# A fused transformer block on one Trainium2 core: when the row-finishing work of the second feed-forward product is issued, and the order of two products in the last up column tile

## The chip, the cores and the metric

The kernel runs on one core of one Trainium2 chip. The metric is the device time of one execution in microseconds. The kernel before took 1763.22 us in the median of three runs (1759.53 to 1764.78).

## The reference, cut to what matters

One hybrid block: a modulated norm, attention and a recurrent mixer, a merge through `w_o`, and then a feed-forward part with a convolution along the rows, all in float32 on 1024 rows by 1024 columns. The change lies in the feed-forward part and the final norm:

```python
def conv_ffn(u, w_up, conv_w, conv_b, w_down):       # u [1024,1024], w_up [1024, 2*2816], w_down [2816,1024]
    a, b = jnp.split(u @ w_up, 2, axis=-1)
    a = lax.conv_general_dilated(a, ...) + conv_b    # width 3, causal, per column
    return (jax.nn.silu(a) * b) @ w_down
...
    h = h + gate2[:, None, :] * conv_ffn(u2, w_up[l], conv_w[l], conv_b[l], w_down[l])
    return rms_norm(h, final_g)                      # per row: y * rsqrt(mean(y*y) + eps) * final_g
```

## The kernel before, in words

**Products.** Every matrix product is done with seven half-size block products (Strassen's scheme in Winograd's form) instead of eight, called P1 to P7 in this document and `k` in the code. Each float32 operand is split into a rounded high part and a rest (`split`: ScalarE casts the high part, line 1298; VectorE subtracts for the rest, line 1301), and one product of operands takes three matmuls (`PARTS`: high by high, low by high, high by low, in this order).

**Up product.** It runs over 22 column tiles (`NFF`), i = 0 to 21. `plan` (lines 1556 to 1560) writes out the order of (tile, product) by hand. For tiles from 3 on this is P1, P7, then P3 of the tile before, then P6, P2, P4, P5. P1, P6, P5 and P3 of a tile add up in one PSUM bank, called X; P7 and P4 in the bank Y; P2 in W. `up_evac` reads a bank after a product: after P6 a copy U of X is taken (line 1510), after P4 `U = Y + U` (line 1515), after P5 `Z = X + Z` (line 1517, reading X), after P3 X is copied (line 1519) and fed to the convolution (lines 1478, 1475, 1482). P3 writes X again, so it must come after line 1517 has read it. In tiles up to 20, P1 and P7 of the next tile lie between P5 and P3; in tile 21 nothing does.

**Second product.** `ORDER = (1, 7, 6, 4, 5, 2, 3)` is the order of its seven block products, called stages s = 0 to 6. Each stage has 11 units (`NP`), so there are 77 units, u = 0 to 76. A unit is 12 matmuls: for each of four row blocks `tp`, three matmuls into that row block's bank. `dn_load` issues a unit's loads on the DMA queue of SyncE, `dn_make` its casts and subtractions; `dn_ahead(u + 8, u + 5)` keeps loads up to eight units and operands up to four units ahead of the unit that is multiplied. Operands lie in a ring of ten buffers (`RING`), two per unit, so the casts of unit u + 4 wait until TensorE has finished unit u - 1. The first units' loads and operands are made during tile 21 of the up product, by a table of `dn_ahead` arguments that is indexed by the product just finished.

**Order on the engines.** From line 1666 on the instructions of all engines stand in the order in which the program issues them. Each engine takes its own in that order.

**Finishing the rows.** The right half rows 512 to 1023 (`R`) are complete after stage 4. `row_sum` (VectorE lines 1758 and 1759, then ScalarE's squares with row sums, line 1760, and `rms_rstd`, lines 280 and 281) and `row_out` (VectorE line 1765, then the store, line 1766) finish one of four row blocks each. In stage 5 they are issued alternately, after units j = 1 to 8. Rows 0 to 511 have their left columns complete after stage 5 (`dn_evac`, line 1746); `first_left` (VectorE lines 1772 and 1773, ScalarE line 1774, VectorE lines 1775 and 1776) does one row block of these after each of the units j = 1 to 4 of stage 6.

**The last stage.** In stage 6 only the first `own = NP - 5`, that is six, units run unit by unit. The other five (u = 72 to 76) run row block by row block: 15 matmuls of row block 0, then `last_right(0)`, then 15 of row block 1, and so on. `last_right` is a chain through VectorE and ScalarE (lines 1782 to 1788) and ends with two stores.

Of the kernel before, what the change touches and what calls it, by code (L numbers as in the profile page):

```python
# [11 lines left out]
AF = mybir.ActivationFunctionType  # L12
ALU = mybir.AluOpType
# [5 lines left out]
NH = 512  # L19
FF = 2816  # L20
NFF = FF // 128
NP = NFF // 2
# [109 lines left out]
def hybrid_block(ctx: ExitStack, tc: tile.TileContext, a, out):  # L132
    nc = tc.nc
# [15 lines left out]
    tt, stt, ts = nc.vector.tensor_tensor, nc.vector.scalar_tensor_tensor, nc.vector.tensor_scalar  # L149
# [128 lines left out]
    def rms_rstd(dst, ssq):  # L278

        nc.scalar.activation(dst, ssq, AF.Ln, scale=1.0 / D, bias=epsr[:, 0:1])  # L280
        nc.scalar.activation(dst, dst, AF.Exp, scale=-0.5)
# [46 lines left out]
    with ExitStack() as es:  # L328
# [67 lines left out]
        with tc.tile_pool(name="st", bufs=1) as st, tc.tile_pool(name="stp", bufs=2, space=PS) as stp, \  # L396
                tc.manual_schedule(engines={mybir.EngineType.SP, mybir.EngineType.DVE, mybir.EngineType.Activation}):
            ssq = st.tile([128, 8], F32, name="ssq")
# [589 lines left out]
    with tc.manual_schedule(engines={mybir.EngineType.DVE, mybir.EngineType.Activation}):  # L988
# [6 lines left out]
        def slot(free):  # L995
            while not free:
                yield 100
            yield free.popleft() - weave.now
# [156 lines left out]
    def bank(k, name):  # L1155
        return pb.tile([128, NH], F32, tag="big", name=name) if k > 5 else pz.tile([128, NH], F32, tag=f"p{k}", name=name)
# [58 lines left out]
    with ExitStack() as es:  # L1215
# [24 lines left out]
        for n in range(8):  # L1240
            if n > 1:
                br_open(n)
            if n:
                for kt in ((n - 1,), (6, 7))[n == 7]:
                    i = nc.sync.dma_start(wo[kt], a["w_o"][kt * 128 : kt * 128 + 128, :])
# [17 lines left out]
    ssq = hp.tile([128, 32], F32, name="ssq2")  # L1263
# [241 lines left out]
    def up_evac(i, k):  # L1505
        o = ups[i]
        if k in (1, 7, 6):
            key = {1: "x1", 7: "Z", 6: "U"}[k]
            o[key] = hp.tile([128, NH], F32, tag="xq", name=f"{key}_{i}", bufs=5)
            nc.scalar.copy(o[key], o["Y" if k == 7 else "X"])  # L1510
        elif k == 2:
            if i > 1:
                up_first(i)
        elif k == 4:
            o["C21"] = tt(o["U"], o["Y"], o["U"], op=ALU.add)
        elif k == 5:
            o["C22"] = tt(o["Z"], o["X"], o["Z"], op=ALU.add)  # L1517
        else:
            nc.scalar.copy(o["ab"][:, 2 + NH :], o["X"])
            conv_last(i, 1, o["X"])  # L1520
            later(0, conv_taps, i, 1)
            later(1, silu, i, 1)
            later(2, gated, i, 1)
# [32 lines left out]
    plan = [(i, k) for ks in ((1, 2), (7,), (6,)) for i in range(2) for k in ks]  # L1556
    plan += [(0, 4), (0, 5), (1, 4), (1, 5), (0, 3), (1, 3)] + [(2, k) for k in (1, 7, 6, 2, 4, 5)]
    for i in range(3, NFF):
        plan += [(i, 1), (i, 7), (i - 1, 3)] + [(i, k) for k in (6, 2, 4, 5)]
    plan.append((NFF - 1, 3))  # L1560
    done = {"made": 0, "run": 0}

# [70 lines left out]
    for n in range(4):  # L1633
        i, k = next(steps)
# [49 lines left out]
    def dn_load(u):  # L1684
        k, j = units[u]
        if j % 2 == 0:
            n, w, r = AS.index(OPS[k][0]), min(2, NP - j), GR[dn["g"] % len(GR)]
            dn["g"] += 1
            graw[k, j] = rp.tile([128, 1024], F32, tag="raw", name=f"g{k}_{j}") if r[0] == "r" else slot(r, f"g{k}_{j}")
            nc.sync.dma_start(graw[k, j][:, 0 : w * NH].rearrange("p (j n) -> p j n", n=NH), d_g[n, :, j : j + w, :])  # L1690
        if k in (1, 7, 4):
            x, cs = {1: (0, slice(0, D)), 7: (1, slice(NH, D)), 4: (1, slice(0, NH))}[k]
            if (j, x) not in wd:
                wd[j, x] = slot(WR[x][j], f"wd{2 * j + x}")
            i = 2 * j + x
            nc.sync.dma_start(wd[j, x][:, cs], a["w_down"][i * 128 : i * 128 + 128, cs])
# [6 lines left out]
    def dn_ahead(loads, makes):  # L1703
        while dn["loaded"] < min(len(units), loads):
            dn_load(dn["loaded"])
            dn["loaded"] += 1
        while dn["made"] < min(len(units), makes):
            dn_make(dn["made"])
            dn["made"] += 1

    def dn_make(u):

        k, j = units[u]
        first, other = W_(j, "B11"), W_(j, "B12")
        if k in (7, 6, 4):
            x, y = {7: (W_(j, "B22"), other), 6: (W_(j, "B22"), first), 4: (W_(j, "B21"), other)}[k]
            tt(other, x, y, op=ALU.subtract)
            w = other
        else:
            w = first if k in (1, 5) else W_(j, OPS[k][1])  # L1720
        for x, src in enumerate((G_(k, j), w)):
            op = slot(RING[(2 * u + x) % 10], f"op{u}{x}", F32R)
            split(op[:, 0:NH], op[:, NH:], src, nc.vector)
            dn_ops[u, x] = op[:, 0:NH], op[:, NH:]
        if k == 1:
            tt(first, other, first, op=ALU.subtract)

    def dn_mm(u, tp, ps):
        k, j = units[u]
        (gs, ws) = (dn_ops[u, x] for x in range(2))  # L1730
        for n, (xi, wi) in enumerate(PARTS):
            mm(ps, gs[xi][:, tp * 128 : tp * 128 + 128], ws[wi], start=k in FRESH and j == 0 and n == 0,
               stop=j == NP - 1 and n == 2, more=k not in FRESH)

    def dn_evac(k, tp, ps):
        if k == 1:
            nc.scalar.copy(XT[tp], ps)
        elif k == 7:
            nc.scalar.copy(R[tp][:, NH:], ps)
        elif k == 6:  # L1740
            nc.scalar.copy(R[tp][:, 0:NH], ps)
        elif k in (4, 5):
            c = R[tp][:, 0:NH] if k == 4 else R[tp][:, NH:]
            tt(c, ps, c, op=ALU.add)
        elif k == 2:
            tt(XT[tp], ps, XT[tp], op=ALU.add)
        else:
            last_right(tp, ps)

    def h_back(t, tag):  # L1750
        H[t] = slot(tag, f"h{t}_")
        nc.sync.dma_start(H[t], d_h[t])
# [1 line left out]


    def row_sum(tp):
        t, x = 4 + tp, R[tp]
        tt(x, x, g2b, op=ALU.mult)
        tt(x, x, H[t], op=ALU.add)
        nc.scalar.activation(H[t], x, AF.Square, accum_out=ssq[:, t : t + 1])  # L1760
        rms_rstd(ssq[:, 16 + t : 17 + t], ssq[:, t : t + 1])

    def row_out(tp):
# [6 lines left out]
    def first_left(t):  # L1770
        x, h = XT[t], H[t][:, 0:NH]
        tt(x, x, g2b[:, 0:NH], op=ALU.mult)
        tt(h, h, x, op=ALU.add)
        nc.scalar.activation(x, h, AF.Square, accum_out=ssq[:, t : t + 1])
        ts(ssq[:, t : t + 1], ssq[:, t : t + 1], 1.0 / D, RMS_EPS, op0=ALU.mult, op1=ALU.add)
        tt(x, h, fgb[:, 0:NH], op=ALU.mult)

# [15 lines left out]
    for i, k in steps:  # L1793
        up_evac(i, k)
        if i == NFF - 1:
            dn_ahead(*{1: (0, 0), 7: (4, 0), 6: (4, 0), 2: (5, 1), 4: (6, 2), 5: (7, 3), 3: (8, 4)}[k])
    while due:
        done["run"] += 1
        run_due()
# [6 lines left out]
    XT = [slot(k, f"xt{k}") for k in ("b7", "e5")]  # L1806
    XT = [XT[tp // 2][:, tp % 2 * NH : tp % 2 * NH + NH] for tp in range(4)]
    R = [slot(f"h{4 + tp}", f"r{tp}") for tp in range(4)]
    H = {}
    banks = [bank(k, f"D{k}") for k in (2, 3, 4, 6, 0, 7, 5, 1)]  # L1810
    for s, k in enumerate(ORDER):
        ps = banks[4:] if k in (7, 4, 2) else banks[0:4]
        own = NP - 5 if s == 6 else NP
        for j in range(own):
            u = s * NP + j
            dn_ahead(u + 8, u + 5)
            for tp in range(4):
                dn_mm(u, tp, ps[tp])
            if s == 4 and j in (5, 6, 7, 8):
                h_back(j - 1, f"h{j - 5}")  # L1820
            if s == 5 and j < 4:
                h_back(j, f"m{12 + j}")
            if s == 5 and 1 <= j <= 8:
                (row_sum if j % 2 else row_out)((j - 1) // 2)
            if s == 6 and 1 <= j <= 4:
                first_left(j - 1)
        if s == 3:
            fgb = slot("e1", "fgb")
            nc.sync.dma_start(fgb, a["final_g"].to_broadcast([128, D]))
        if s == 6:  # L1830
            dn_ahead(len(units), len(units))
        for tp in range(4):
            for j in range(own, NP):
                dn_mm(s * NP + j, tp, ps[tp])
            dn_evac(k, tp, ps[tp])
# [78 lines left out]
```

## Time and profile before

| | us |
|---|---|
| median of three runs (lowest to highest) | 1763.22 (1759.53 to 1764.78) |
| the profiled execution's own time | 1764.5 |
| span of the profiled execution | 1762.4 |
| TensorE busy | 1660.7 (94% of the span) |
| VectorE busy | 1264.8 (72%) |
| ScalarE busy | 818.0 (46%) |
| GpSimd busy | 352.7 (20%), none of it in the stretch of this change |
| first matmul of the second product | 1531.14 after the start of the span |
| end of its last matmul | 1754.90 |

PE is TensorE's matmul, PEld its weight load, DVE is VectorE, ACT is ScalarE, SPq the DMA queue of SyncE. A row of a timeline gives the start and the duration in us, the engine, the line of the source, the operation, the tile written and the tiles read, the shape, the count of instructions merged into the row, and in brackets how long the engine was idle ahead of it and which instruction ended that. `[2.45 <-DVE Z L1517]` is an idle time of 2.45 us that ended when VectorE's line 1517 had written Z. A row of a table by windows gives the stretch, its length, the busy time and count for PE, PEld, DVE, ACT and POOL, then the clock granted to TensorE as a fraction, the busy share of the DMA engines and GB/s.

### The profile page before, as it was taken

To read this page: it belongs to the slowest core of one execution; us is meant where nothing else is said; L and a number is where in the kernel's file an instruction comes from. 1 tells how busy PE (TensorE), PEld (TensorE's weight loads), DVE (VectorE), ACT (ScalarE), POOL (GpSimd) and SP (SyncE) were. 2 spreads that over 40 slices of the span, in tenths; PEclk is the share of its full clock that TensorE was granted. 3 is DMA by queue.
4 is the path that set the end of the run, shared out by engine and by line. 5 is a ranking of instruction groups with operands and counts; after the bars stand their busy time and mean duration, and the time that the engine had idled before them with its cause. 6 is when DMAs were issued, how large, how long until landed. Compare 5 with 4: busy or idle time off the path is not lost.

```text
span 1762.4 us, 26237 instructions
## 1 busy us (share of the span) xinstructions
PE 1660.7 (94%) x9838; PEld 1353.2 (77%) x9838; DVE 1264.8 (72%) x2342; ACT 818.0 (46%) x1502; POOL 352.7 (20%) x249
## 2 busy tenths in 40 slices
PE   7999989999899997999899898999999999999997
PEld 7767767778687776888788777788888888788875
DVE  5765777777867424888649898877777777786576
ACT  5453234434334444767630335744444444445444
POOL 0233222332322222322138473000000000000000
PEclk9999989999999998999999899999999999999998
DMA  8487633442323229444168502122332322574442
GB/s 317 145 294 227 168 100 103 114 114 88 101 93 95 74 78 175 124 112 127 43 233 312 209 22 96 60 90 90 121 113 90 114 92 100 208 241 160 160 151 90
DMA packets 120846, 239.85 MB, mean 136 GB/s; under 512 B 39760, under 2 KB 48208, under 8 KB 120720
## 3 DMA queue, kind: packets, MB, share of 16 engines
q1 hardware_dynamic: 105600, 220.94, 38.4%
q0 software_dynamic: 15120, 17.25, 4.5%
q8 instruction: 77, 1.26, 0.3%
q14 instruction: 49, 0.40, 0.1%
HBM read 172.59 MB, written 65.54 MB: 135 GB/s over the span
## 4 chain that ended last, share of the span: by engine, by line
PE 60%; DVE 22%; DMA 8%; issue 5%; ACT 2%; POOL 1%; SPq 1%; DVEq 0%; ACTq 0%; POOLq 0%
PE X L140 13%; PE D L140 9%; PE Y L140 6%; PE rk_ps L140 4%; PE ps_rkv L140 4%; PE gt L140 3%; PE W L140 3%; DVE E L764 3%; DVE t L762 3%; PE qk L140 2%; PE lg L140 2%; DMA wm<-in_w_mod 2%; PE ov L140 2%; PE tp L144 2%; PE sp L140 1%
## 5 line engine op out<-in xcount | busy, mean ns | idle before, releaser
L140 PE MATMUL D<-op,op 128*128 128x512 f32 x924 | 216.0, 396 | 7.8 <-ACT op L1298 7.5
L140 PEld LDWEIGHTS D<-op,op 128*128 128x128 f32 x924 | 175.7, 191 | 47.9 <-ACT op L1298 8.8
L256 POOL TENSOR_TENSOR lo_in<-raw_in,hi_in 128x1024 fp32r<-128x1024 f32 x48 | 119.8, 2497 | 244.7 <-ACT hi_in L255 70.8
L140 PE MATMUL X<-T,S 128*128 128x512 f32 x528 | 127.1, 390 | 0.8 <-DVE T L1301 0.8
L140 PEld LDWEIGHTS X<-T,S 128*128 128x128 f32 x528 | 99.0, 188 | 21.9 <-DVE T L1301 1.4
L762 DVE TENSOR_TENSOR t<-E,M 128x60 f32<-128x60 f32 (+24 forms) x248 | 79.3, 320 | 29.6 <-DMA M<-sm 23.9
L1301 DVE TENSOR_TENSOR op<-g,op 128x512 fp32r<-128x512 f32 x77 | 53.0, 688 | 53.8 <-ACT op L1298 53.8
L1475 DVE SCALAR_TENSOR_TENSOR c<-ab,vec,c 128x512 f32<-128x512 f32 x88 | 65.9, 749 | 22.5 <-ACT c L1478 21.1
L1298 ACT CAST op<-g 128x512 fp32r<-128x512 f32 x77 | 47.6, 619 | 65.2 <-PE D L140 40.1
L1439 DVE TENSOR_TENSOR S<-ur,S 128x512 fp32r<-128x512 f32 x66 | 45.6, 691 | 39.0 <-ACT S L1435 39.0
L764 DVE TENSOR_TENSOR E<-E,t 128x60 f32<-128x60 f32 (+24 forms) x248 | 67.7, 273 | 5.9
L255 ACT CAST hi_in<-raw_in 128x1024 fp32r<-128x1024 f32 x40 | 41.8, 1046 | 62.3 <-PE ps_rkv L140 25.2
L1439 DVE TENSOR_TENSOR A<-ur,A 128x512 fp32r<-128x512 f32 x66 | 46.4, 704 | 32.2 <-ACT A L1435 32.2
L140 PE MATMUL X<-B,S 128*128 128x512 f32 x264 | 65.0, 397 | 2.5 <-DVE Z L1517 2.5
L140 PE MATMUL Y<-T,S 128*128 128x512 f32 x264 | 64.5, 391 | 2.6 <-ACT T L1298 1.3
L1435 ACT CAST S<-ur 128x512 fp32r<-128x512 f32 x66 | 41.0, 622 | 49.5 <-DVE ur L1426 31.0
L140 PE MATMUL X<-B,A 128*128 128x512 f32 x264 | 63.5, 390 | 0.0
L140 PE MATMUL W<-B,A 128*128 128x512 f32 x264 | 63.5, 390 | 0.0
L140 PE MATMUL Y<-T,A 128*128 128x512 f32 x264 | 63.4, 389 | 0.0
L1435 ACT CAST A<-ur 128x512 fp32r<-128x512 f32 x66 | 41.0, 622 | 47.5 <-PE X L140 41.8
L140 PE MATMUL ps_rkv<-u_hi,hi_in 128*128 128x512 f32 x192 | 54.2, 409 | 7.6 <-DVE r L351 4.0
L1031 ACT ACTIVATE P<-lg,nm 128x896 f32<-128x896 f32 (+3 forms) x64 | 47.4, 743 | 29.3 <-DVE nm L1027 29.1
(611 smaller groups left out, 4243.8 us busy)
## 6 DMA issues: line engine op xcount, KB each, us to landing
raw_in<-in_w_in SPq DMA_DIRECT2D x50, 512.0 KB, 4.7
wm<-in_w_mod SPq DMA_DIRECT2D x48, 512.0 KB, 6.7
ur<-in_w_up SPq DMA_DIRECT2D x44, 512.0 KB, 3.9
g<-d_g SPq DMA_DIRECT2D x35, 512.0 KB, 4.5
d_g<-gs SPq DMA_DIRECT2D x44, 256.0 KB, 2.0
d_g<-c SPq DMA_DIRECT2D x33, 256.0 KB, 4.4
d_st<-qh SPq DMA_DIRECT2D x64, 128.0 KB, 2.4
d_gate<-gs SPq DMA_DIRECT2D x32, 256.0 KB, 2.6
```

The lines of the kernel that those rows point to most:

```text
L140: nc.tensor.matmul(o, lhsT, rhs, start=start, stop=stop, skip_group_check=more)
L144: nc.tensor.transpose(o, i, eye)
L255: nc.scalar.copy(hi, raw)
L256: nc.gpsimd.tensor_tensor(lo, raw, f32(hi), op=ALU.subtract)
L762: tt(tv, E32[:, 0:J, s : s + 1].to_broadcast([128, J, W]), M32[:, s : s + 1, s + 1 : 32].to_broadcast([128, J, W]), op=ALU.mult)
L764: tt(E32[:, 0:J, s + 1 : 32], E32[:, 0:J, s + 1 : 32], tv, op=ALU.add)
L1031: nc.scalar.activation(e[:, 0:n], lg[:, 0:n], AF.Exp, bias=nm[:, 0:1], accum_out=nm[:, 1:2])
L1298: nc.scalar.copy(hi, src)
L1301: eng.tensor_tensor(lo, src, f32(hi), op=ALU.subtract)
L1435: nc.scalar.copy(hi, src)
L1439: tt(lo, src, f32(hi), op=ALU.subtract)
L1475: stt(c, ab[:, x + hf * NH : x + hf * NH + NH], V("conv_w", 22 * x + i), c, op0=ALU.mult, op1=ALU.add)
```

## The change

Four edits, none of which adds or removes work for an engine:

1. In tile 21 of the up product P5 is put ahead of P4: P2, P5, P4, P3 instead of P2, P4, P5, P3. The table of `dn_ahead` arguments is turned with it, so that the same loads and operands come at the same places of the sequence.
2. `row_sum` keeps its two VectorE instructions; squares and `rms_rstd` become `row_norm`. `first_left` keeps its two VectorE instructions; the squares become `first_norm`, the last two VectorE instructions `first_scaled`.
3. The steps of one row block are spread over the units. In stage 5: `row_sum(t)` after unit j = 1 + 2t, `row_norm(t)` after 2 + 2t, `row_out(t)` after 4 + 2t. In stage 6: `first_left(t)` after j = 1 + t, `first_norm(t)` after 2 + t, `first_scaled(t)` after 3 + t. Each step is issued behind the operands that are made in the same step of the loop.
4. In stage 6 seven units instead of six run unit by unit (`own = NP - 4`), so four units (u = 73 to 76) run row block by row block, 12 matmuls each.

In the changed kernel the lines below the diff move: 1760 becomes 1763, 1765 becomes 1768, 1772 and 1773 become 1775 and 1776, 1774 becomes 1779, 1775 and 1776 become 1783 and 1784, 1782 to 1788 become 1790 to 1796.

```diff
     for i in range(3, NFF):
-        plan += [(i, 1), (i, 7), (i - 1, 3)] + [(i, k) for k in (6, 2, 4, 5)]
+        plan += [(i, 1), (i, 7), (i - 1, 3)] + [(i, k) for k in ((6, 2, 4, 5) if i < NFF - 1 else (6, 2, 5, 4))]
...
     def row_sum(tp):
-        t, x = 4 + tp, R[tp]
+        x = R[tp]
         tt(x, x, g2b, op=ALU.mult)
-        tt(x, x, H[t], op=ALU.add)
-        nc.scalar.activation(H[t], x, AF.Square, accum_out=ssq[:, t : t + 1])
+        tt(x, x, H[4 + tp], op=ALU.add)
+
+    def row_norm(tp):
+        t = 4 + tp
+        nc.scalar.activation(H[t], R[tp], AF.Square, accum_out=ssq[:, t : t + 1])
         rms_rstd(ssq[:, 16 + t : 17 + t], ssq[:, t : t + 1])
...
         tt(h, h, x, op=ALU.add)
-        nc.scalar.activation(x, h, AF.Square, accum_out=ssq[:, t : t + 1])
+
+    def first_norm(t):
+        nc.scalar.activation(XT[t], H[t][:, 0:NH], AF.Square, accum_out=ssq[:, t : t + 1])
+
+    def first_scaled(t):
+        x, h = XT[t], H[t][:, 0:NH]
         ts(ssq[:, t : t + 1], ssq[:, t : t + 1], 1.0 / D, RMS_EPS, op0=ALU.mult, op1=ALU.add)
         tt(x, h, fgb[:, 0:NH], op=ALU.mult)
...
-            dn_ahead(*{1: (0, 0), 7: (4, 0), 6: (4, 0), 2: (5, 1), 4: (6, 2), 5: (7, 3), 3: (8, 4)}[k])
+            dn_ahead(*{1: (0, 0), 7: (4, 0), 6: (4, 0), 2: (5, 1), 5: (6, 2), 4: (7, 3), 3: (8, 4)}[k])
...
+    finish = {}
+    for t in range(4):
+        for n, f in ((1 + 2 * t, row_sum), (2 + 2 * t, row_norm), (4 + 2 * t, row_out), (NP + 1 + t, first_left),
+                     (NP + 2 + t, first_norm), (NP + 3 + t, first_scaled)):
+            finish.setdefault(5 * NP + n, []).append((f, t))
     for s, k in enumerate(ORDER):
         ps = banks[4:] if k in (7, 4, 2) else banks[0:4]
-        own = NP - 5 if s == 6 else NP
+        own = NP - 4 if s == 6 else NP
...
-            if s == 5 and 1 <= j <= 8:
-                (row_sum if j % 2 else row_out)((j - 1) // 2)
-            if s == 6 and 1 <= j <= 4:
-                first_left(j - 1)
+            for f, t in finish.get(s * NP + j, ()):
+                f(t)
```

## The prediction

> **What bounds the kernel now.** I read the page first, then TensorE's waits from 1500 us on, then timelines of single engines.
>
> ```profile
> span 1762.4 us, 26237 instructions
> L140 PE MATMUL D<-op,op 128*128 128x512 f32 x924 | 216.0, 396 | 7.8 <-ACT op L1298 7.5
> g<-d_g SPq DMA_DIRECT2D x35, 512.0 KB, 4.5
> ```
> ```profile
> PE D L140 <- ACT op L1298: 7.5, 3, 2.6
> PE X L140 <- DVE Z L1517: 2.5, 1, 2.5
> ```
>
> TensorE is the bound of the whole stretch: these four are all the waits that the view lists from 1500 us on, so whatever the change wins comes out of them and of what they drag along. The timeline of TensorE shows where they lie.
>
> ```profile
> 1518.63 2.88 PE L140 MATMUL Y<-T,A 128*128 128x512 f32 x12
> 1521.35 2.88 PE L140 MATMUL X<-T,S 128*128 128x512 f32 x12
> 1526.69 4.61 PE L140 MATMUL X<-B,S 128*128 128x512 f32 x12 [2.45 <-DVE Z L1517]
> 1531.14 1.08 PE L140 MATMUL D<-op,op 128*128 128x512 f32 x4
> ```
> ```profile
> 1689.74 24.32 PE L140 MATMUL D<-op,op 128*128 128x512 f32 x106
> 1716.34 2.25 PE L140 MATMUL D<-op,op 128*128 128x512 f32 x6 [2.28 <-ACT op L1298]
> ```
> ```profile
> 1740.88 14.02 PE L140 MATMUL D<-op,op 128*128 128x512 f32 x51 [2.61 <-ACT op L1298]
> ```
> ```profile
> 1526.69:1531.30 4.61, 4.61 (x13) 3.67 (x14) 1.84 (x3) 0.01 (x1) 0.00 (x0) 0.63 0.72 275
> 1700.00:1713.90 13.90, 13.90 (x62) 11.16 (x60) 11.16 (x13) 4.65 (x11) 0.00 (x0) 1.00 0.45 149
> ```
>
> Twelve matmuls take 2.72 us at full pace (1521.35 less 1518.63), the last of them ending 0.16 later (2.88). In the windows the granted clock, third figure from the end, is 1.00 in one where nothing is waited for and 0.63 in the one behind the wait for line 1517. So a wait costs its own length and a slow spell after it.
>
> **Part 1, P5 ahead of P4.** P3 follows P5 and could have started at 1521.35 + 2.72 = 1524.07. It started 2.62 later, at 1526.69, for line 1517, and took 1531.14 - 1526.69 = 4.45 instead of 2.72, which is 1.73 of slow spell. VectorE's timeline shows why line 1517 came late, though its bank was complete at 1521.35 + 2.88 = 1524.23 (left out are operands of the second product and taps of the convolution, which run without idle time):
>
> ```profile
> 1521.97 0.68 DVE L1515 TENSOR_TENSOR U<-Y,U 128x512 f32<-128x512 f32 x1
> ...
> 1525.95 0.68 DVE L1517 TENSOR_TENSOR Z<-X,Z 128x512 f32<-128x512 f32 x1
> ...
> 1533.14 0.69 DVE L1301 TENSOR_TENSOR op<-g,op 128x512 fp32r<-128x512 f32 x1 [4.58 <-ACT op L1298]
> ```
>
> The edit exchanges lines 1515 and 1517 in this queue. P5 then ends at 1518.63 + 2.88 = 1521.51, so line 1517 runs at 1521.97 and is done at 1522.65, while P4 holds TensorE until 1524.07. P3 starts then, without a wait. Line 1515 takes the place at 1525.95, behind P4's end (1524.23); the convolution's gate that reads U comes only after the row at 1533.14. The loads keep their places in the DMA queue, as the table of loads was turned too. Gain: 2.62 + 1.73 = 4.35 us.
>
> What is late next? The row at 1533.14 belongs to unit 3, and the operands of units 3 and 4 hang on P3's end through ScalarE (its copy, the convolution, the casts). VectorE idled 4.58 us ahead of it. With P3 earlier by 4.35 it is due at 1528.79, and VectorE is free at 1533.14 - 4.58 = 1528.56. The chain moves as a whole, with 0.23 us in hand, so I count the 4.35 in full.
>
> **Part 2, the steps behind the operands.** First what stands to be won. From 1531.14 to the end of the last matmul, 1740.88 + 14.02 = 1754.90, are 223.76 us. The 924 matmuls need 924 / 12 x 2.72 + 0.16 = 209.60. The stage loses 14.16. The wait at 1716.34 ended a run that stopped at 1689.74 + 24.32 = 1714.06; less 0.16, that is 182.76 after the start, or 67 units (182.24) and 0.52. So units 0 to 66 lose 0.52, which stays, and 13.64 lies from unit 67 on: 7.5 in the three waits, the rest in slow spells and in matmuls held up singly.
>
> Why does unit 67 wait? VectorE in stage 5:
>
> ```profile
> 1690.68 0.69 DVE L1301 TENSOR_TENSOR op<-g,op 128x512 fp32r<-128x512 f32 x1 [2.29 <-ACT op L1298]
> 1691.29 0.68 DVE L1301 TENSOR_TENSOR op<-wd,op 128x512 fp32r<-128x512 f32 x1
> 1691.89 1.28 DVE L1765 SCALAR_TENSOR_TENSOR h__15169<-r,ssq,fgb 128x1024 f32<-128x1024 f32 x1
> 1693.09 0.68 DVE L1301 TENSOR_TENSOR op<-g,op 128x512 fp32r<-128x512 f32 x1
> 1693.69 0.68 DVE L1301 TENSOR_TENSOR op<-wd,op 128x512 fp32r<-128x512 f32 x1
> 1694.30 1.21 DVE L1758 TENSOR_TENSOR r<-r,g2b 128x1024 f32<-128x1024 f32 x1
> 1695.54 1.23 DVE L1759 TENSOR_TENSOR r<-r,h__15191 128x1024 f32<-128x1024 f32 x1
> 1699.06 0.69 DVE L1301 TENSOR_TENSOR op<-g,op 128x512 fp32r<-128x512 f32 x1 [2.29 <-ACT op L1298]
> ```
>
> The casts of the next unit stand behind the squares on ScalarE, and these behind line 1759. So VectorE stands 2.29 us in each pair of units, and a pair takes 1699.06 - 1690.68 = 8.38 against TensorE's 5.44. With the squares one unit later the next unit's casts are ahead of them, and VectorE's own work remains: 1.21 for a unit's two subtractions (1690.68 to 1691.89), 1.20 for line 1765 (to 1693.09), 2.45 for the pair of sums (1694.30, plus 1.24, plus about 1.21). A pair of units: 2 x 1.21 + 1.20 + 2.45 = 6.07. That is still over 5.44, but only by 0.63, and the four units of lead carry it.
>
> I follow the queue through, on the clock of the trace before (part 1 moves all of it). Unit 67 then starts at 1531.14 + 182.76 = 1713.90, unit 72 at 1727.50; the row-wise part begins with units 73, 74, 75 and 76 at 1730.22, 1730.90, 1731.58 and 1732.26. VectorE is free at 1690.68 - 2.29 = 1688.39 and subtracts for unit 61 to 1689.60. Unit 62 still has to wait for the first squares, to 1690.68, and is done at 1691.89. From there nothing is idle: sums 1694.34, unit 63 and line 1765 1696.75, unit 64 and sums 1700.41, unit 65 and 1765 1702.82, unit 66 and sums 1706.48, unit 67 1707.69. That is 6.2 us ahead of need. Line 1765, units 68 and 69, line 1765: 1712.51. Stage 6 has its own rows:
>
> ```profile
> 1720.62 1.28 DVE L1746 TENSOR_TENSOR xtb<-D,xtb 128x512 f32<-128x512 f32 x2
> 1721.82 1.28 DVE L1746 TENSOR_TENSOR xte<-D,xte 128x512 f32<-128x512 f32 x2
> ```
> ```profile
> 1725.42 0.68 DVE L1772 TENSOR_TENSOR xtb<-xtb,g2b 128x512 f32<-128x512 f32 x1
> 1726.13 0.69 DVE L1773 TENSOR_TENSOR h__15295<-h__15295,xtb 128x512 f32<-128x512 f32 x1
> 1727.61 0.15 DVE L1775 TENSOR_SCALAR ssq<-ssq 128x1 f32<-128x1 f32 x1 [0.79 <-ACT xtb L1774]
> 1727.68 0.68 DVE L1776 TENSOR_TENSOR xtb<-h__15295,fgb 128x512 f32<-128x512 f32 x1
> 1728.28 0.69 DVE L1301 TENSOR_TENSOR op<-g,op 128x512 fp32r<-128x512 f32 x1
> ```
>
> The four of line 1746 take 2.40 (1.20 from pair to pair); a row's steps took 1728.28 - 1725.42 = 2.86, of which 1.42 are lines 1772 and 1773 (0.71 each) and 0.67 lines 1775 and 1776 (1727.61 to 1728.28). With a unit's 1.21 that made 4.07; without the idle time it is 3.30. On from 1712.51: line 1746 1714.91, units 70 and 71 1717.33, first row 1718.75, unit 72 1719.96, second row 1721.38, unit 73 1722.59, then 0.67 and 1.42 to 1724.68, unit 74 1725.89, again to 1727.98, unit 75 1729.19, 0.67, unit 76 1731.07. Each is ahead of its start above; the narrowest is unit 76, by 1.2 us. So no wait is left and all 13.64 go.
>
> The stores of line 1766 move two units back in SyncE's DMA queue; behind the last (at 1712.51) stands the load for units 74 and 75, whose casts cannot start before unit 69 is multiplied, at 1722.06. That leaves 9.5 us for a load that takes 4.5 in the page's row: cost nothing.
>
> **Part 3, rows of 12 matmuls.** The end is a chain of row blocks:
>
> ```profile
> 1751.53 0.68 DVE L1782 TENSOR_TENSOR o<-D,g2b 128x512 f32<-128x512 f32 x1
> ...
> 1754.30 0.75 DVE L1787 SCALAR_TENSOR_TENSOR o<-h__15342,ssq,fgb 128x512 f32<-128x512 f32 x1 [1.35 <-ACT ssq L1786]
> 1754.96 0.69 DVE L1782 TENSOR_TENSOR o<-D,g2b 128x512 f32<-128x512 f32 x1
> ```
>
> Line 1782 of a row stands behind line 1787 of the row before, so the chain can't go faster than 1754.96 - 1751.53 = 3.43 a row. Fifteen matmuls are 3.40, so before, the chain ended with TensorE: 1754.96 is 0.06 after its end. Twelve are 2.72, and the chain falls back by 0.71 in each of three rows. That costs 2.13 us, with nothing to hide it.
>
> **Sum.** -4.35 - 13.64 + 2.13 = -15.86. The profiled execution took 1764.5 with a span of 1762.4; it becomes 1748.6 with a span of 1746.5. Taken from the median of the runs, 1763.22, this gives 1747.3.
>
> **A rule weighed.** The Trainium skill, "TensorE: Matmul & The Clock Gate", Part 1, has the clock halved after an idle window of about 3.4 us. The wait ahead of P3, 2.45 us, is shorter, and the window shows a granted clock of 0.63 behind it all the same, so I go by the window; by the page the slow spells would not be the waits' doing, and the sum would be that of (a) below.
>
> **The rivals.**
> (a) *The slow spells stay.* If the clock drops for another reason, only the waits go: 2.62 + 7.5 - 2.13 = 8.0, so 1755.2. Against it: 1.00 in the window without a wait. 3%.
> (b) *Unit 4 is no earlier.* If something other than P3's end holds the chain of part 1 (0.23 us in hand), the 4.35 come back as a wait for its operands: 1751.7. 7%.
> (c) *Unit 76 is late.* Were the VectorE steps 0.1 us longer than their rows, the 1.2 in hand would be gone over the 16 units, and row block 0 would stand for 1 to 2 us with up to 1.73 of slow spell behind it: up to 1751.0. 7%.
> (d) *The steps don't come apart.* If ScalarE still holds casts behind squares and a pair keeps its 8.38, only parts 1 and 3 count: -2.2, so 1761.0. The queue order speaks against it. 4%.
> (e) *Slower: the load behind the last store.* If it landed after 1722.06, TensorE would stop ahead of the row-wise part, one for one and 1.73 for the clock. It decides only from 9.5 us on; a loss over 5.3 needs a load of about 15.86 + 5.3 + 9.5 - 1.73 = 29 us, against 4.5. 3%, mostly for what I haven't seen.
>
> **How the numbers follow.** The forecast has 76%. A measurement of this kernel can tell about 0.3%, 5.3 us, from no change. The forecast, (a), (b) and (c) are all faster by more: 0.93. (d) is within: 0.04. (e): 0.03. The range takes in the forecast, (b) and (c) and the spread of the runs before (3.7 below the median, 1.6 above): 1743.5 to 1753.0.
>
> **What would show it.** In the changed profile line 1517 runs ahead of P4's end, P3's 12 matmuls take 2.88 without a wait, and the second product begins near 1526.8. From 1680 us on TensorE has no wait over 0.3 us and a granted clock of 1.00. Its last matmul ends near 1737, and the span goes on for 9.6 us instead of 7.5, with line 1790 at intervals of 3.43. I am wrong if a wait for line 1298 or 1301 stands in stage 6, or if the second product begins earlier and loses it again by unit 4.

## The result, and the profile after

The changed kernel took 1744.06 us in the median of four runs (1743.83 to 1745.21), the kernel before 1761.38 in the median of four (1759.24 to 1764.78). The ratio is 0.9901, with a 95% interval of 0.9882 to 0.9921: 17.3 us faster. Forecast were 1747.3 us and 15.9 us less.

First two rows of the page after, then TensorE's timeline from the product behind P2 to the end, and the window of the second product (PE, PEld, DVE, ACT and POOL busy, then the granted clock, the share of the DMA engines and GB/s).

```profile
span 1742.0 us, 26232 instructions
...
L140 PE MATMUL D<-op,op 128*128 128x512 f32 x924 | 210.1, 390 | 0.0
```
```profile
1514.20 2.88 PE L140 MATMUL X<-T,S 128*128 128x512 f32 x12
1516.92 2.88 PE L140 MATMUL Y<-T,A 128*128 128x512 f32 x12
1519.64 2.88 PE L140 MATMUL X<-B,S 128*128 128x512 f32 x12
1522.36 210.14 PE L140 MATMUL D<-op,op 128*128 128x512 f32 x924
```
```profile
1522.36:1732.50 210.14, 210.14 (x925) 173.34 (x923) 160.83 (x248) 106.19 (x198) 0.00 (x0) 1.00 0.52 173
```

All 924 matmuls now stand in one row: TensorE is never idle from P2 of tile 21 to the last matmul, and its clock is 1.00 throughout. The span can be cut into three stretches that no work ahead of the change enters: A, from the start of the product behind P2 to the first matmul of the second product; B, the second product; C, from its last matmul to the end of the span.

| us | start of A | A | B | C | A + B + C |
|---|---|---|---|---|---|
| before | 1518.63 | 12.50 | 223.76 | 7.5 | 243.7 |
| forecast change | | -4.35 | -13.64 | +2.13 | -15.86 |
| after | 1514.20 | 8.16 | 210.14 | 9.5 | 227.8 |
| measured change | | -4.34 | -13.62 | +2.05 | -15.91 |

The changes are taken before rounding. The span fell by 20.4 us, since A also began 4.4 us earlier. That is not the change's: in thirteen profiles of this study the start of A lies between 1509.66 and 1522.43, and the instructions ahead of it are the same, apart from the order of two casts and their subtractions in tile 21. The spread arises ahead of the up product: from the first matmul into the bank X to the start of A, all thirteen took 395.6 to 395.8 us. The earliest start has the least time at half clock ahead of it (44 us from 20 us on), and the two latest the most (72 us each); that the clock makes the spread is not shown. It is why the experiments are compared by their stretches, and why the time of one run says little about differences of a few us.

VectorE around the exchanged products, and in stage 5:

```profile
1517.54 0.68 DVE L1517 TENSOR_TENSOR Z<-X,Z 128x512 f32<-128x512 f32 x1
...
1521.52 0.68 DVE L1515 TENSOR_TENSOR U<-Y,U 128x512 f32<-128x512 f32 x1
...
1524.37 0.69 DVE L1301 TENSOR_TENSOR op<-g,op 128x512 fp32r<-128x512 f32 x1 [0.24 <-ACT op L1298]
```
```profile
1681.92 0.69 DVE L1301 TENSOR_TENSOR op<-g,op 128x512 fp32r<-128x512 f32 x1 [1.08 <-ACT op L1298]
1682.53 0.69 DVE L1301 TENSOR_TENSOR op<-wd,op 128x512 fp32r<-128x512 f32 x1
1683.13 1.22 DVE L1758 TENSOR_TENSOR r<-r,g2b 128x1024 f32<-128x1024 f32 x1
1684.38 1.23 DVE L1759 TENSOR_TENSOR r<-r,h__15191 128x1024 f32<-128x1024 f32 x1
1685.52 0.69 DVE L1301 TENSOR_TENSOR op<-g,op 128x512 fp32r<-128x512 f32 x1
1686.12 0.69 DVE L1301 TENSOR_TENSOR op<-wd,op 128x512 fp32r<-128x512 f32 x1
1686.73 1.28 DVE L1768 SCALAR_TENSOR_TENSOR h__15169<-r,ssq,fgb 128x1024 f32<-128x1024 f32 x1
1687.92 0.69 DVE L1301 TENSOR_TENSOR op<-g,op 128x512 fp32r<-128x512 f32 x1
```

Line 1517 is done at 1518.22, ahead of P3's start at 1519.64, and the operands of unit 3 now find VectorE idle for 0.24 us instead of 4.58; the forecast had 0.23. From the first sums of stage 5 on, the one idle time left in that stage is the 1.08 us ahead of unit 62, and line 1768 stands between two units without waiting for ScalarE. The tail, VectorE again:

```profile
1724.32 0.69 DVE L1790 TENSOR_TENSOR o<-D,g2b 128x512 f32<-128x512 f32 x1 [1.92 <-PE D L140]
...
1727.76 0.68 DVE L1790 TENSOR_TENSOR o<-D,g2b 128x512 f32<-128x512 f32 x1
...
1731.19 0.68 DVE L1790 TENSOR_TENSOR o<-D,g2b 128x512 f32<-128x512 f32 x1
...
1734.62 0.68 DVE L1790 TENSOR_TENSOR o<-D,g2b 128x512 f32<-128x512 f32 x1
```

Only the first row block waits for TensorE. The others follow at 3.43 us, and the last begins at 1734.62, 2.1 us after the last matmul.

### The profile page after: what moved, and what is told of

Same layout as the page of the kernel before. It is cut to its first block, busy times and chain, and to the rows that moved or that the text cites. A ratio compares the mean times of both kernels' runs of the same rounds, so it can differ in the third digit from the quotient of the medians.

```text
span 1742.0 us, 26232 instructions
## 1 busy us (share of the span) xinstructions
PE 1654.0 (95%) x9838; PEld 1351.8 (78%) x9838; DVE 1264.3 (73%) x2342; ACT 819.5 (47%) x1502; POOL 352.1 (20%) x249
## 4 chain that ended last, share of the span: by engine, by line
PE 61%; DVE 21%; DMA 8%; issue 5%; ACT 2%; SPq 2%; POOL 1%; DVEq 0%; ACTq 0%; POOLq 0%
PE X L140 14%; PE D L140 12%; PE Y L140 7%; PE rk_ps L140 4%; PE W L140 3%; DVE E L764 3%; PE gt L140 3%; DVE t L762 3%; PE ps_rkv L140 3%; DMA wm<-in_w_mod 2%; PE lg L140 2%; PE ov L140 2%; PE tp L144 2%; PE tr L140 2%; PE qk L140 1%
## 5 line engine op out<-in xcount | busy, mean ns | idle before, releaser
L140 PE MATMUL D<-op,op 128*128 128x512 f32 x924 | 210.1, 390 | 0.0
L762 DVE TENSOR_TENSOR t<-E,M 128x60 f32<-128x60 f32 (+24 forms) x248 | 75.1, 303 | 27.6 <-DMA M<-sm 21.9
L764 DVE TENSOR_TENSOR E<-E,t 128x60 f32<-128x60 f32 (+24 forms) x248 | 72.0, 290 | 5.9
```

The costliest lines, as they stand in the source:

```text
L140: nc.tensor.matmul(o, lhsT, rhs, start=start, stop=stop, skip_group_check=more)
L762: tt(tv, E32[:, 0:J, s : s + 1].to_broadcast([128, J, W]), M32[:, s : s + 1, s + 1 : 32].to_broadcast([128, J, W]), op=ALU.mult)
L764: tt(E32[:, 0:J, s + 1 : 32], E32[:, 0:J, s + 1 : 32], tv, op=ALU.add)
```

## The experiments

**P5 ahead of P4 alone** (the kernel before with edit 1).

```diff
-        plan += [(i, 1), (i, 7), (i - 1, 3)] + [(i, k) for k in (6, 2, 4, 5)]
+        plan += [(i, 1), (i, 7), (i - 1, 3)] + [(i, k) for k in ((6, 2, 4, 5) if i < NFF - 1 else (6, 2, 5, 4))]
...
-            dn_ahead(*{..., 4: (6, 2), 5: (7, 3), ...}[k])
+            dn_ahead(*{..., 5: (6, 2), 4: (7, 3), ...}[k])
```

> The kernel before with P5 ahead of P4 in tile 21 alone. Theory (each wait costs its length and a slow spell): from the start of the product after P2 to the first matmul of the second product 8.16 us instead of 12.51; the second product's matmuls then take 223.8 us as before and the tail 7.5. Time 4.35 us under before (ratio 0.9975). Rival (the operands of unit 4 hold the start): the first stretch is 8.16 too, but the second product takes about 228 us and the time does not change.

TensorE's timeline:

```profile
1514.49 2.88 PE L140 MATMUL X<-T,S 128*128 128x512 f32 x12
...
1522.65 182.94 PE L140 MATMUL D<-op,op 128*128 128x512 f32 x804
1707.88 17.86 PE L140 MATMUL D<-op,op 128*128 128x512 f32 x66 [2.29 <-ACT op L1298]
1728.35 1.47 PE L140 MATMUL D<-op,op 128*128 128x512 f32 x3 [2.62 <-ACT op L1298]
1732.42 13.98 PE L140 MATMUL D<-op,op 128*128 128x512 f32 x51 [2.60 <-ACT op L1298]
```

A is 1522.65 - 1514.49 = 8.16, B 223.75, C 7.5 (span 1753.9): 4.4 us less, and the three waits of the second product are untouched, the first again after exactly 804 matmuls, that is ahead of unit 67. The rival falls: nothing comes back by unit 4. The times alone could not tell (ratio 0.9990, 0.9973 to 1.0007).

**Rows of 12 alone** (the kernel before with edit 4).

```diff
-        own = NP - 5 if s == 6 else NP
+        own = NP - 4 if s == 6 else NP
```

> The kernel before with seven instead of six units of stage 6 unit by unit (rows of 12 matmuls), nothing else. Theory: VectorE's steps set when row block 0 is done, so it is done no earlier than before; three rows of 12 instead of 15 then end TensorE's work about 2 us earlier (second product 221.7 us), and the chain of rows takes it back (tail 9.5 instead of 7.5): time within 1 us of before. Rival (the rows of 15 cause the two waits of 2.61 us in stage 6): these waits go, the second product takes about 217 us, and the time falls by 4 us or more.

```profile
1534.79 182.99 PE L140 MATMUL D<-op,op 128*128 128x512 f32 x804
1720.08 19.31 PE L140 MATMUL D<-op,op 128*128 128x512 f32 x75 [2.30 <-ACT op L1298]
1740.55 1.46 PE L140 MATMUL D<-op,op 128*128 128x512 f32 x3 [1.16 <-ACT op L1298]
1744.62 11.82 PE L140 MATMUL D<-op,op 128*128 128x512 f32 x42 [2.61 <-ACT op L1298]
```

B is 1744.62 + 11.82 - 1534.79 = 221.65, C 9.0 (span 1765.4). TensorE ends 2.1 us earlier and the tail is 1.5 longer, where 2.0 was expected: 0.6 less together, and the ratio of the times is 1.0004 (0.9984 to 1.0023). The edit shortens one wait, from 2.61 to 1.16 us, but removes none; VectorE's steps decide when row block 0 is done.

**The steps spread in one stage only** (the changed kernel with the parts of a row put together again in the other).

```diff
-... (1 + 2 * t, row_sum), (2 + 2 * t, row_norm), (4 + 2 * t, row_out), (NP + 1 + t, first_left), (NP + 2 + t, first_norm), (NP + 3 + t, first_scaled)
+... (1 + 2 * t, row_sum), (2 + 2 * t, row_norm), (4 + 2 * t, row_out), (NP + 1 + t, first_left), (NP + 1 + t, first_norm), (NP + 1 + t, first_scaled)   # stage 5 only
+... (1 + 2 * t, row_sum), (1 + 2 * t, row_norm), (2 + 2 * t, row_out), (NP + 1 + t, first_left), (NP + 2 + t, first_norm), (NP + 3 + t, first_scaled)   # stage 6 only
```

> The changed kernel with the steps spread in stage 5 only; in stage 6 the three parts of a row block stand together again, as before. Theory (leads worked out from the queue): unit 67 has no wait; stage 6 goes at 4.07 us a unit on VectorE from unit 72 on, so units 75 and 76 are late in row block 0 by 1 to 2 us; second product 212 to 215 us. Rival (stage 6 alone makes its two waits of 2.61 us, whatever lead it starts with): second product about 217 us with waits of 2.6 us.

> The changed kernel with the steps spread in stage 6 only; in stage 5 row_norm stands behind row_sum and row_out in the next unit, as before. Theory: unit 67 waits 2.3 to 2.5 us as in the trace before, with a slow spell after it, and stage 6 starts without lead, so unit 76 is late by about 2 us too: second product 216 to 218 us. Rival (the waits of stage 6 are made in stage 6 alone): only the wait at unit 67 is left, second product 210.1 + 2.4 + 1.7 = 214.2 us.

TensorE's timeline, stage 5 only and then stage 6 only:

```profile
1517.82 200.55 PE L140 MATMUL D<-op,op 128*128 128x512 f32 x882
1719.27 12.48 PE L140 MATMUL D<-op,op 128*128 128x512 f32 x42 [0.90 <-ACT op L1298]
```
```profile
1520.26 182.94 PE L140 MATMUL D<-op,op 128*128 128x512 f32 x804
1705.48 21.75 PE L140 MATMUL D<-op,op 128*128 128x512 f32 x82 [2.29 <-ACT op L1298]
1727.42 9.35 PE L140 MATMUL D<-op,op 128*128 128x512 f32 x38 [0.18 <-DVE op L1301]
```

With stage 5 alone B is 213.93, with stage 6 alone 216.50, each within the theory's range and away from its rival. In the second, unit 67 waits as in the trace before (2.4 us late, and 2.1 of slow spell). The late unit 76 there is no wait of 2 us, though: matmuls of units 75 and 76 in row block 0 are held up one by one, 1.7 us in all and 0.18 the longest wait. Both versions have the rows of 12, so their gains count from the 221.65 us of that edit alone: 7.7 for stage 5, 5.1 for stage 6 and 11.5 for both. The two overlap by 1.4 us. That fits the lead: with stage 5 spread, the steps that stand together in stage 6 cost 3.8 us, and with stage 5 bunched they cost 5.1.

**Rows of 15 in the changed kernel.**

```diff
-        own = NP - 4 if s == 6 else NP
+        own = NP - 5 if s == 6 else NP
...
             dn_ahead(len(units), len(units))
+            for f, t in finish[s * NP + own]:
+                f(t)
```

> The changed kernel with rows of 15 matmuls in stage 6 as before; the last scaling step is issued behind the last unit's operands. Theory: the tail is 7.5 us instead of 9.5, and row block 0 waits 0.5 to 1 us for unit 76, without a slow spell: second product 210.7 to 211.2 us, time about 1 us under the changed kernel. Rival (rows of 12 are needed for the gain): the waits in row block 0 come back with a slow spell, second product 212.5 to 214.5 us, time 0 to 2 us over the changed kernel.

```profile
1525.28 210.28 PE L140 MATMUL D<-op,op 128*128 128x512 f32 x924
```
```profile
1723.43 0.69 DVE L1301 TENSOR_TENSOR op<-g,op 128x512 fp32r<-128x512 f32 x1
1724.03 0.69 DVE L1301 TENSOR_TENSOR op<-wd,op 128x512 fp32r<-128x512 f32 x1
```

C is 7.5 as forecast (span 1743.0), but the wait for unit 76 did not come: B is 210.28, and 210.21 in a second profile further below, as against 210.14 and 210.21 in the two of the changed kernel. The rows of VectorE show unit 76's operands at 1724.12 and 1724.72. In the forecast's walk they are done at 1731.07 on the clock of the trace before, which is 1725.21 on this one (the second product begins 5.86 earlier). The walk was 0.5 us pessimistic, which is more than half of the 0.85 us by which it has unit 76 late: with rows of 15 that unit begins at 1727.50 + 4 x 0.68 = 1730.22, against 1731.07.

**The last scaling one row block later.**

```diff
     def last_right(t, ps):
...
-        stt(x, h, r, fgb[:, NH:], op0=ALU.mult, op1=ALU.mult)
         nc.scalar.activation(XT[t], XT[t], AF.Copy, scale=r)
+        if t:
+            last_out(t - 1)          # the scaling and the right half's store of the row block before
...                                   # store of the left half
+        if t == 3:
+            last_out(t)
```

> The changed kernel with the last scaling of each row block (VectorE's line 1795 and its store) issued behind the two VectorE instructions of the next row block, so that the chain of row blocks is no longer one after the other. Theory (line 1795 in VectorE's queue makes the interval of 3.43 us): row blocks come at TensorE's 2.72 us, the tail is 7.5 us instead of 9.5, the second product stays at 210.1, time 2.0 us under the changed kernel. Rival (ScalarE's chain or the stores set the end): the tail stays at 9 us or more.

VectorE at the end (the second product runs here from 1527.71 for 210.14 us, to 1737.85):

```profile
1732.42 0.69 DVE L1790 TENSOR_TENSOR o<-D,g2b 128x512 f32<-128x512 f32 x1 [1.32 <-PE D L140]
...
1735.16 0.69 DVE L1790 TENSOR_TENSOR o<-D,g2b 128x512 f32<-128x512 f32 x1 [0.66 <-PE D L140]
...
1737.89 0.69 DVE L1790 TENSOR_TENSOR o<-D,g2b 128x512 f32<-128x512 f32 x1 [0.66 <-PE D L140]
```

Each row block now waits for TensorE, at intervals of 2.73, and C is 7.5 (span 1745.3). So the tail's 2 us were line 1795 in VectorE's queue ahead of the next row block's first instruction, and neither ScalarE nor the stores.

**The three on one chip**, for the time.

> The changed kernel itself, for a comparison on one chip with the next two: 16 us under the kernel before (ratio 0.991); second product 210.1 us, tail 9.5.

> The changed kernel with rows of 15, a second time: second product 210.3 us, tail 7.5, 1.9 us under the changed kernel (ratio to before 0.990), if the stretch ahead of the change lasts alike.

> The changed kernel with the last scaling one row block later, a second time: second product 210.1 us, tail 7.5, 2.0 us under the changed kernel (ratio to before 0.990), if the stretch ahead of the change lasts alike.

| | median | ratio to before | 95% interval | B | C |
|---|---|---|---|---|---|
| changed | 1743.85 | 0.9907 | 0.9886 to 0.9927 | 210.21 | 9.5 |
| rows of 15 | 1742.09 | 0.9889 | 0.9866 to 0.9911 | 210.21 | 7.5 |
| scaling later | 1742.51 | 0.9895 | 0.9873 to 0.9916 | 210.21 | 7.5 |

Both variants are 1.9 to 2.2 us under the changed kernel in B + C, in each of their two profiles. Their medians here lie 1.8 and 1.3 under it; the intervals overlap, so the times alone don't show it. Nor did the first four runs of each, with medians of 1744.45 for rows of 15 and 1746.28 for the later scaling against the 1744.06 of the changed kernel.

**What a wait costs.** ScalarE gets copies from a tile at rest into a spare one, ahead of one unit's casts, at six places of stages 1 to 4.

```diff
+    HOLD = {(1, 1): 23, (1, 8): 24, (2, 5): 25, (3, 2): 26, (3, 9): 28, (4, 2): 32}    # second run: 16, 19, 18, 20, 26, 23
...
+            if (s, j) in HOLD:
...
+                for n in range(HOLD[s, j]):
+                    nc.scalar.copy(idle[:, n % 2 * NH : n % 2 * NH + NH], g2b[:, 0:NH])
```

> The changed kernel with copies added on ScalarE in stages 1 to 4 (23, 24, 25, 26, 28 and 32 of 128x512 from a tile at rest to a spare one, nothing left out), each lot ahead of one unit's casts, so that TensorE waits once after each lot, by about 0.52 us for each copy less 11.2 us: 0.8, 1.3, 1.8, 2.3, 3.4 and 5.4 us where the lead is full, up to 3 us more where it isn't. Theory (a wait brings a slow spell behind it): the spells of matmuls at 0.427 us follow the longer waits, from somewhere under 2.4 us on, and last 3 to 4 us, so a wait costs its length and 1.6 to 1.8 us. Rival (only a whole idle window of about 3.4 us halves the clock): no slow matmul behind the waits under 3.4 us, and a spell of about 3.4 us behind the longer ones.

The waits came out longer than planned, at 3.5 to 7.7 us, so nothing lay under 3.4 and the theories stayed undivided: a spell of 6 to 12 matmuls at 0.427 us followed each. Hence the second run.

> The kernel with added copies on ScalarE again, with fewer of them (16, 19, 18, 20, 26 and 23), so that TensorE waits about 0.4, 1.2, 1.9, 2.2, 2.5 and 3.0 us, all under 3.4. Theory (a wait well under 3.4 us already halves the clock for some 3 us): spells of 7 or more matmuls at 0.427 us behind the waits from about 1 us on, none behind the shortest. Rival (the windows are fixed in time and a wait needs to fill one): no such spell behind any of them, and the waits of the trace before had theirs for another reason.

Not all of its waits came as planned either: in order they lasted 0.74, 3.31, 1.69, 4.17, 3.94 and 2.33 us instead of 0.4, 1.2, 1.9, 2.2, 2.5 and 3.0. TensorE's timeline of the second run, and the 4 us behind four of the waits with the granted clock third from the end:

```profile
1572.47 19.71 PE L140 MATMUL D<-op,op 128*128 128x512 f32 x84 [0.74 <-ACT op L1298]
1595.49 23.93 PE L140 MATMUL D<-op,op 128*128 128x512 f32 x96 [3.31 <-ACT op L1298]
1621.12 22.43 PE L140 MATMUL D<-op,op 128*128 128x512 f32 x96 [1.69 <-ACT op L1298]
1647.72 20.73 PE L140 MATMUL D<-op,op 128*128 128x512 f32 x84 [4.17 <-ACT op L1298]
1672.39 13.80 PE L140 MATMUL D<-op,op 128*128 128x512 f32 x48 [3.94 <-ACT op L1298]
1688.52 75.37 PE L140 MATMUL D<-op,op 128*128 128x512 f32 x324 [2.33 <-ACT op L1298]
```
```profile
1572.47:1576.50 4.03, 3.94 (x16) 3.06 (x17) 3.86 (x7) 2.27 (x5) 0.00 (x0) 1.00 0.38 130
1595.49:1599.50 4.01, 3.92 (x10) 2.93 (x11) 3.85 (x7) 2.25 (x5) 0.00 (x0) 0.57 0.45 131
1621.12:1625.20 4.08, 4.00 (x16) 3.11 (x17) 3.91 (x8) 2.32 (x5) 0.00 (x0) 1.00 0.69 210
1688.52:1692.50 3.98, 3.98 (x11) 3.06 (x12) 3.98 (x8) 3.98 (x8) 0.00 (x0) 0.61 0.42 80
```

Behind 0.74 and 1.69 us the clock stays at 1.00, and the next 28 matmuls lose 0.5 us (single ones held up by VectorE's half of the operand). Behind 2.33 us it is at 0.61 and they lose 1.6; behind the 3.31 and more, 1.5 to 2.8. So here a wait has its price. The theory had spells from about 1 us on; behind 1.69 us there was none.

The length of the wait alone does not decide, though. In each of the thirteen traces the granted clock is 1.00 or 0.50 and changes only at moments that lie whole multiples of 3.41 us apart; in the stretch of this change a spell lasts one such window or two. These are the windows between such moments around the waits of 1.69 and 2.33 us, and then around the wait of 0.90 us in the version with stage 5 only:

```profile
1616.56:1619.97 3.41, 2.87 (x13) 2.05 (x11) 0.00 (x0) 3.41 (x8) 0.00 (x0) 1.00 0.00 0
1619.97:1623.38 3.41, 2.18 (x8) 1.61 (x9) 2.72 (x5) 2.49 (x6) 0.00 (x0) 1.00 0.28 49
1623.38:1626.80 3.42, 3.42 (x16) 2.82 (x15) 3.33 (x6) 1.74 (x4) 0.00 (x0) 1.00 1.05 365
1684.83:1688.24 3.41, 1.36 (x6) 0.78 (x5) 0.26 (x1) 3.41 (x8) 0.00 (x0) 1.00 0.00 0
1688.24:1691.65 3.41, 3.13 (x7) 2.36 (x8) 3.41 (x7) 3.41 (x8) 0.00 (x0) 0.50 0.27 36
```
```profile
1718.14:1721.55 3.41, 2.31 (x8) 0.97 (x7) 3.16 (x6) 2.12 (x5) 0.00 (x0) 1.00 0.00 0
1721.55:1724.97 3.42, 3.42 (x9) 2.65 (x10) 1.40 (x3) 1.24 (x5) 0.00 (x0) 0.50 0.00 0
```

The wait of 1.69 us lay across two windows, 0.55 us in one and 1.15 in the next; of the 2.33 us, 2.05 lay in one window, and the whole window behind it is at 0.50. With 0.90 us, single matmuls held up in the same window did the rest. I count as idle whatever a window at full clock has beyond its matmuls at pace (0.227 us each, that is 2.72 / 12). From 1505 us to the last matmul of all thirteen traces, each such window with 2.09 us of idle time or more was followed by one at half clock (24 of them), and none with 1.93 us or less was. Of the rival for the second run, then, the windows fixed in time hold; that a wait must fill one does not. The Trainium skill, "TensorE: Matmul & The Clock Gate", Part 1, puts an idle window of about 3.4 us ahead of the halving; here a window of 3.41 us that was idle for 2.09 was enough, and the measurement decides.

## Why the prediction was right

- *TensorE is the bound, and only its waits can be won*: held. With its waits gone B is 210.14, which is the 209.60 of 924 matmuls at pace and the 0.5 us that the forecast left in.
- *Part 1, 4.35 us*: 4.34, in the changed kernel and alone. That the chain behind P3 moves as a whole also held, with the 0.24 us of idle time to show for it.
- *Part 2, 13.64 us*: 13.62. The walk through VectorE's queue named what each stage would do, and the two half versions split as it says. Its one error is small: unit 76 was ready some 0.5 us earlier than reckoned. A row's lines 1772 and 1773 (1775 and 1776 in the changed kernel) took 1.34 instead of 1.42 (1708.33 to 1709.67 in the trace after), and the pair of sums 2.39 instead of 2.45 (1683.13 to 1685.52). It didn't count in the changed kernel, and it did for rows of 15.
- *Part 3, 2.13 us*: 2.05, and its cause is shown by the version that moves line 1795. The cost belongs to a kernel whose waits are gone: with the steps bunched, the same edit gains 0.6 us (rows of 12 alone). So rival (d), which kept the waits and still charged the 2.13, was put some 2.7 us too high.
- *The slow spells as part of a wait's cost*: held. They went with the waits, which fells rival (a), for which only 8.0 us would have gone, and the added copies bring them back. It held for waits of 2.3 us and more; that each wait has its spell is too simple, since the idle time of one clock window decides.
- *The time*: 17.3 us measured against 15.9, within the interval (0.9882 to 0.9921 is 20.8 to 13.9 us). The span fell further, 20.4, for the stretch ahead of the change, which the forecast had no reason to move and which varies by itself. For the same reason the two moments that it named, 1526.8 and 1737, came 4.4 us early (1522.36 and 1732.50). The three stretches give 15.9.

## What to carry to other kernels

Where two engines take turns (casts on one, subtractions on the other), a step that goes back and forth between them belongs a unit behind the operands made in the same turn, so that neither queue holds the next unit's operands behind an answer from the other; the saved lead is then spent in the next stage too. Walk the slower queue through with the intervals of its own rows, not the durations, before counting on it. A tail of dependent row blocks has its own interval: compare it with the matmuls per row block before choosing how many there are, or move the instruction that stands in the next row block's way.

## What was not expected of the hardware

- The clock goes to half for whole windows of 3.41 us, one behind the other on a fixed grid, after a window in which TensorE was idle for 2.09 us or more, single hold-ups counted; with 1.93 us or less it did not. So a wait of 1.69 us across two windows had no spell behind it (5 to 12 matmuls at 0.427 us), and one of 0.90 us among hold-ups had one.
- The start of A lies between 1509.66 and 1522.43 us in thirteen profiles, while A, B and C repeat to 0.15 us between kernels that are alike there.
